# Seven block products instead of eight in two chunks of each feed-forward

## The chip, the core and the metric

One core of a Trainium2 chip runs the whole program: a launch, six transformer layers of two kinds on 256 tokens of width 1024, one output. The metric is device time in microseconds from start to end of an execution; the lower, the better. The engines of the core that matter here are TensorE (PE in the profile, with its weight loads as PEld), VectorE (DVE), ScalarE (ACT), GpSimd (POOL) and SyncE (SP), which issues nearly all loads. Each runs its own instructions in the order in which the program gives them, and waits on semaphores for the others.

## The reference, cut to what matters

The program is four layers of a first kind (mixer by short convolution, pooling or differential attention, then a feed-forward) and two of a second kind (feed-forward, mixer, feed-forward): eight feed-forwards in all. Only they change. Each is, with a root-mean-square norm ahead of it and one behind it:

```python
def _swiglu(xn, w_gate, w_up, w_down):
    return (jax.nn.silu(xn @ w_gate) * (xn @ w_up)) @ w_down
```

`xn` is 256 x 1024, `w_gate` and `w_up` are 1024 x 2816, `w_down` is 2816 x 1024, all float32.

## The kernel before, in words

A float32 product is made of three matmuls on float32r operands: every operand is split into a high part (a cast, ScalarE) and a low part (operand minus high part, VectorE), and `mm3` (line 184) adds high x high, high x low and low x high in PSUM. One matmul has a 128x128 stationary operand (tokens of one half, 128 values of k) and 128x512 moving weights; so one `mm3` is three matmuls, at lines 187 to 189.

Tokens are two halves of 128. `to_T` (line 268) transposes a half of x on TensorE, multiplies by the norm's gain (line 277) and splits it (`split`, line 193) into `xT`, a pair of large buffers; the norm's per-token factor is applied later, at the eviction of a product from PSUM.

Weights come in pieces of 128x2048 floats (1 MB; 4 blocks of k by 512 columns, or 2 by 1024 for the down product). All pieces of the program stand in one list, in the order of use (`plan_ffn`, line 321). `load_step` (line 105) issues the loads on SyncE, up to `raw_max` = 3 unsplit pieces ahead, while more than `spare` = 2 of the 19 large buffers `r8` are free. `split_step` (line 118) splits half a piece: a cast at line 134 and a subtraction at line 135. Two such steps turn a raw piece into a pair of buffers, and the raw buffer goes back.

What sets the order is `tick` (line 156): the program is written out by one thread that walks through TensorE's work, and after each `mm3` it takes one `split_step` and lets waiting tasks go on whose tick has come. A split that is not forced happens only if no `hold` is set, the piece is at most `ahead` pieces further than the one in use, fewer than `limit` pieces are split and live, and two buffers are free. `hold` is set from the end of a half's mixer or feed-forward until that half's `to_T` has been issued. `spawn(gen, n)` puts a task n ticks later, `join` forces one, `need` forces a split.

A feed-forward (`ffn`, line 337) goes through six chunks of the 2816 columns, five of 512 and one of 256. For chunk c, `gate_up(c, h)` makes gate and up of one token half in two PSUM banks (16 `mm3` each), evicts them with a Silu on ScalarE (line 368) and a product on VectorE (line 369), and spawns the task `T`, eleven ticks later, which transposes the 128x512 result on TensorE (line 375) and splits it (lines 196 and 197). `down(c, h)` multiplies it with the chunk's rows of `w_down` into two banks per half that stay open over all chunks. The loop's order is gate and up of half 0, down of the chunk before for half 1, gate and up of half 1, down of this chunk for half 0. PSUM has eight banks, and four of them are the down product's.

Behind a feed-forward or mixer, `chain` (line 296) and `post` (line 238) make the norm and the residual on ScalarE, VectorE and a power on GpSimd (line 216).

Of the kernel before, what the change touches and what calls it, by code (L numbers as in the profile page):

```python
# [27 lines left out]
ORD = "VQKvco"  # L28

# [20 lines left out]
class Core:  # L50
    def __init__(self, ctx, tc, I, out):
# [21 lines left out]
        self.raw, self.hl, self.xt = {}, {}, {}  # L73
        self.raw_max = 3
        self.spare = 2
        self.hold = 0
        self.rr = {}
# [17 lines left out]
    def add(self, *srcs):  # L95

        self.pieces.append(srcs)
        return len(self.pieces) - 1

    def view(self, t, i):  # L100
        srcs = self.pieces[i]
        kt, n = srcs[0].shape[1], sum(s.shape[2] for s in srcs)
        return t[:, 0:kt * n].rearrange("p (k n) -> p k n", k=kt)

    def load_step(self, most=10 ** 9):
        while self.n_dma < most and self.n_dma < len(self.pieces) and len(self.r8.free) > self.spare and len(self.raw) < self.raw_max:
# [8 lines left out]
            self.raw[i] = t  # L115
            self.n_dma += 1

    def split_step(self, force=False, eng=None):
        i = self.n_split
        if i >= len(self.pieces):  # L120
            return False
        if self.sub == 0:
            if not force and (self.hold or i > self.cur + self.ahead or self.live >= self.limit or len(self.r8.free) < 2):
                return False
            self.load_step()
            if i not in self.raw:
                return False
            self.hl[i] = (self.r8.get(), self.r8.get())
            self.live += 1
        hi, lo = (self.view(t, i) for t in self.hl[i])  # L130
        k = lo.shape[1]
        sl = slice(0, k // 2) if self.sub == 0 else slice(k // 2, k)
        raw = self.view(self.raw[i], i)[:, sl]
        self.nc.scalar.copy(out=hi[:, sl], in_=raw)  # L134
        (eng or self.nc.vector).tensor_tensor(out=lo[:, sl], in0=raw, in1=hi[:, sl].bitcast(F32), op=ALU.subtract)  # L135
        self.sub += 1
        if self.sub == 2:
            self.sub = 0
            self.r8.put(self.raw.pop(i))
            self.n_split += 1  # L140
            self.load_step()
        return True

    def need(self, i):
        self.cur = max(self.cur, i)
        while self.n_split <= i:
            assert self.split_step(force=True), ("no buffer for piece", i, self.n_dma, self.n_split, len(self.raw), self.raw_max, len(self.r8.free), self.sub)
        return tuple(self.view(t, i) for t in self.hl[i])
# [35 lines left out]
    def mm3(self, out, x, w, first, last, tick=True):  # L184

        mm = self.nc.tensor.matmul
        mm(out=out, lhsT=x[0], rhs=w[0], start=first, stop=False)  # L187
        mm(out=out, lhsT=x[0], rhs=w[1], start=False, stop=False)  # L188
        mm(out=out, lhsT=x[1], rhs=w[0], start=False, stop=last)  # L189
# [66 lines left out]
    def scale_of(self, h):  # L256
# [5 lines left out]
        def rest():  # L262
            r = self.sb.tile([128, 4], F32, tag=f"rr{h}", name=f"rr{h}", bufs=2)
            self.rstd(sx, 2, EPS, r)
            self.rr[h] = r[:, 1:2]
        return rest

    def to_T(self, h, gT, rest, late):
# [12 lines left out]
        for n, z in enumerate(zs):  # L281
            dst = [t[:, 0:2048].rearrange("p (k t) -> p k t", k=8)[:, 4 * n:4 * n + 4, h * 128:(h + 1) * 128] for t in self.xT]
            self.split(dst[0], dst[1], z.rearrange("p (k t) -> p k t", k=4))
            self.f2.put(z)
# [5 lines left out]
        self.spawn(last(), 3 if late else 0)  # L290
        yield
# [18 lines left out]
    def start(self, h, nxt, wait=None, late=False):  # L310
        rest = (lambda: self.scale_of(h)()) if late else self.scale_of(h)
# [4 lines left out]
        else:  # L316
            self.hold += 1
            self.xt[h] = self.spawn(self.to_T(h, self.gT, rest, late), 6 if wait is None else wait)


    def plan_ffn(self, wg, wu, wd):

        G, Dn = [], []
# [3 lines left out]
        for c in range(6):  # L327
            lo = c * 512
            if c < 5:
                G.append([self.add(w[:, 4 * q:4 * q + 4, lo:lo + 512]) for w in (gk, uk) for q in range(2)])  # L330
                Dn.append([self.add(dk[:, 4 * c + 2 * q:4 * c + 2 * q + 2, :]) for q in range(2)])
# [1111 lines left out]
```

## Time and profile before

| | |
|---|---|
| median of 3 runs | 2162.37 us (2160.11 to 2163.01) |
| the profiled execution | 2164.11 us |
| its span, first to last instruction | 2162.3 us |
| mean granted TensorE clock | 0.997 |
| busy share of TensorE, VectorE, ScalarE | 99%, 57%, 49% |
| one load of 1 MB, issue to landing | 5.1 us |

The rows further down are of this execution. In a timeline a row gives the start (us from the span's start), the time, the engine, the line, the operation, output and inputs, with a count where neighbours were merged, and in brackets how long the engine was idle before it and who released it. A matmul's row is its whole way through the array; matmuls overlap, so their cost is the distance of two starts.

### The profile page before, as it was taken

Reading aid. Unit: us, or ns where it says so; the run is one execution under the profiler, and the core shown is the slowest. Engines: PE = TensorE matmul, PEld = TensorE weight load, DVE = VectorE, ACT = ScalarE, POOL = GpSimd, SP = SyncE. Lnnn points to the kernel's source line nnn. Section 1 sums busy time; section 2 is a strip of 40 time slices with the busy share of each in tenths; the row PEclk is TensorE's granted clock in tenths of the full one; section 3 lists DMA queues with packets and bytes.
Section 4 is the critical chain, followed back from the end, with each engine's and each line's share of the span. In section 5 each row is a group of like instructions: output and inputs, shape, how many; then the busy total and the mean of one; then the engine's idle time right before and its main releaser. Section 6 shows DMA issues by size and latency. Waiting matters only on the chain.

```text
span 2162.3 us, 24820 instructions
## 1 busy us (share of the span) xinstructions
PE 2138.5 (99%) x9845; PEld 1729.2 (80%) x9845; DVE 1237.1 (57%) x1664; ACT 1066.4 (49%) x1566; POOL 82.2 (4%) x130
## 2 busy tenths in 40 slices
PE   9999999999999999999999999999999999999998
PEld 6878877887888888888888887878888888787886
DVE  6655475546665456655464554785456446477454
ACT  5554454444664435553454446764435345676342
POOL 1000010000010000000000001000000001000000
PEclk9999999999999999999999999999999999999999
DMA  8555545455454554554654554354554645345541
GB/s 295 188 201 197 190 166 179 171 196 186 137 197 163 200 189 161 210 179 156 213 189 170 193 181 142 118 193 167 196 191 150 214 171 171 128 165 175 175 176 59
DMA packets 175620, 383.73 MB, mean 177 GB/s; under 512 B 10428, under 2 KB 29116, under 8 KB 175504
## 3 DMA queue, kind: packets, MB, share of 16 engines
q1 hardware_dynamic: 172592, 372.04, 50.2%
q0 software_dynamic: 2624, 9.58, 1.2%
q8 instruction: 77, 1.26, 0.2%
q10 hardware_dynamic: 288, 0.52, 0.1%
q14 instruction: 39, 0.32, 0.0%
HBM read 380.28 MB, written 1.84 MB: 177 GB/s over the span
## 4 chain that ended last, share of the span: by engine, by line
PE 93%; DVE 3%; ACT 2%; issue 1%; POOL 1%; DMA 0%; SPq 0%; POOLq 0%; DVEq 0%; ACTq 0%
PE ps L189 29%; PE ps L188 29%; PE ps L187 29%; PE ps L206 2%; PE ps L375 2%; ACT r L134 1%; DVE r L135 1%; PE ps L1042 1%; ACT c_junk L220 1%; PE ps L687 0%; PE ps L732 0%; PE ps L783 0%; PE ps L1016 0%; ACT f L1029 0%; DMA r<-in_conv_w_in_dram 0%
## 5 line engine op out<-in xcount | busy, mean ns | idle before, releaser
L187 PE MATMUL ps<-r,r 128*128 128x512 f32 (+2 forms) x2816 | 1129.5, 401 | 2.6 <-ACT r L196 1.7
L188 PE MATMUL ps<-r,r 128*128 128x512 f32 (+2 forms) x2816 | 1108.1, 394 | 2.5 <-POOL r L135 1.4
L189 PE MATMUL ps<-r,r 128*128 128x512 f32 (+2 forms) x2816 | 1109.5, 394 | 0.1
L135 DVE TENSOR_TENSOR r<-r,r 128x1024 fp32r<-128x1024 f32 (+1 forms) x701 | 815.1, 1216 | 147.0 <-ACT r L134 140.3
L134 ACT CAST r<-r 128x1024 fp32r<-128x1024 f32 x702 | 686.0, 1041 | 194.7 <-PE ps L188 166.8
L189 PEld LDWEIGHTS ps<-r,r 128*128 128x128 f32 (+1 forms) x2816 | 528.2, 188 | 127.1 <-DVE r L197 3.8
L188 PEld LDWEIGHTS ps<-r,r 128*128 128x128 f32 (+1 forms) x2816 | 529.3, 188 | 119.3 <-DVE r L135 3.0
L187 PEld LDWEIGHTS ps<-r,r 128*128 128x128 f32 (+1 forms) x2816 | 529.3, 188 | 118.8 <-ACT r L196 2.2
L369 DVE SCALAR_TENSOR_TENSOR f<-ps,rr,f 128x512 f32<-128x512 f32 (+1 forms) x96 | 67.8, 706 | 458.6 <-PE ps L189 434.4
L196 ACT CAST r<-ps 128x512 fp32r<-128x512 f32 (+1 forms) x108 | 59.9, 555 | 456.2 <-PE ps L375 448.1
L197 DVE TENSOR_TENSOR r<-ps,r 128x512 fp32r<-128x512 f32 (+1 forms) x108 | 70.2, 651 | 189.4 <-ACT r L196 189.4
L368 ACT ACTIVATE f<-ps,rr 128x512 f32<-128x512 f32 (+1 forms) x96 | 62.6, 653 | 156.9 <-PE ps L189 156.8
L216 POOL TENSOR_TENSOR st<-st,c_mhalf 128x1 f32<-128x1 f32 x28 | 15.9, 569 | 1575.7 <-DVE st L215 1574.9
L220 ACT ACTIVATE c_junk<-x 128x512 bf16<-128x512 f32 x56 | 35.3, 631 | 51.3 <-DVE x L253 50.2
L375 PEld LDWEIGHTS ps<-c_ident,f 128*128 128x128 f32 x352 | 44.4, 140 | 13.1
L375 PE MATMUL ps<-c_ident,f 128*128 128x128 f32 x352 | 54.0, 272 | 0.0
L277 DVE TENSOR_TENSOR f<-ps,c_pre 128x512 f32<-128x512 f32 x52 | 33.8, 687 | 29.5 <-PE ps L206 29.3
L196 ACT CAST r<-f 128x512 fp32r<-128x512 f32 x52 | 31.7, 621 | 26.1 <-DVE f L277 26.0
L253 DVE SCALAR_TENSOR_TENSOR x<-f,st,x 128x512 f32<-128x512 f32 x56 | 39.6, 749 | 2.5 <-POOL st L216 0.9
L245 DVE TENSOR_TENSOR f<-ps,gn 128x512 f32<-128x512 f32 x52 | 35.5, 684 | 6.4 <-ACT c_junk L220 6.4
L220 ACT ACTIVATE c_junk<-ps 128x512 bf16<-128x512 f32 x52 | 31.0, 596 | 15.2 <-PE ps L189 14.4
L197 DVE TENSOR_TENSOR r<-f,r 128x512 fp32r<-128x512 f32 x52 | 35.6, 722 | 4.6 <-ACT r L196 2.5
(177 smaller groups left out, 749.3 us busy)
## 6 DMA issues: line engine op xcount, KB each, us to landing
r<-in_ffn_w_in_dram SPq DMA_DIRECT2D x80, 1024.0 KB, 5.2
r<-in_ffn_w_down_dram SPq DMA_DIRECT2D x44, 1024.0 KB, 5.0
r<-in_ffn_w_out_dram SPq DMA_DIRECT2D x44, 1024.0 KB, 5.1
r<-in_ffn_w_gate_dram SPq DMA_DIRECT2D x40, 1024.0 KB, 5.1
r<-in_ffn_w_up_dram SPq DMA_DIRECT2D x40, 1024.0 KB, 5.1
r<-in_mix_w_in_dram SPq DMA_DIRECT2D x28, 1024.0 KB, 5.1
r<-in_conv_w_in_dram SPq DMA_DIRECT2D x22, 1024.0 KB, 5.3
r<-in_attn_w_qkv_dram SPq DMA_DIRECT2D x12, 1024.0 KB, 5.2
```

The costliest lines, as they stand in the source:

```text
L134: self.nc.scalar.copy(out=hi[:, sl], in_=raw)
L135: (eng or self.nc.vector).tensor_tensor(out=lo[:, sl], in0=raw, in1=hi[:, sl].bitcast(F32), op=ALU.subtract)
L187: mm(out=out, lhsT=x[0], rhs=w[0], start=first, stop=False)
L188: mm(out=out, lhsT=x[0], rhs=w[1], start=False, stop=False)
L189: mm(out=out, lhsT=x[1], rhs=w[0], start=False, stop=last)
L196: self.nc.scalar.copy(out=hi, in_=src)
L197: self.nc.vector.tensor_tensor(out=lo, in0=src, in1=hi.bitcast(F32), op=ALU.subtract)
L206: self.nc.tensor.transpose(out=b[:, j * 128:(j + 1) * 128], in_=src[:, j * 128:(j + 1) * 128], identity=self.ident)
L220: self.nc.scalar.activation(out=self.junk[:, 0:src.shape[-1]], in_=src, func=ACTF.Square, scale=scale, accum_out=acc)
L368: self.nc.scalar.activation(out=s[:, 0:n], in_=gb, func=ACTF.Silu, scale=rr[h])
L369: self.nc.vector.scalar_tensor_tensor(out=s[:, 0:n], in0=ub, scalar=rr[h], in1=s[:, 0:n], op0=ALU.mult, op1=ALU.mult)
L375: self.nc.tensor.transpose(out=b[:, j * 128:(j + 1) * 128], in_=s[:, j * 128:(j + 1) * 128], identity=self.ident)
```

## The change: block products and the order of the chunks

In chunks 1 and 3 of each feed-forward gate and up are made together, as a product of two 2x2 block matrices: a11, a12, a21, a22 are the two token halves by the two halves of k, b11 and b21 the two k halves of the gate's weights, b12 and b22 of the up weights. Seven block products replace eight:

```
s1 = a21' , s2, s3, s4 : four differences of input blocks (x_sums, once per feed-forward)
t1 = b11+b12   t2 = t1+b22   t3 = b12+b22   t4 = t2+b21     (all blocks with the signs of s)
products: a11 b11, a12 b21, s1 t1, s2 t2, s4 b22, s3 t3, a22 t4, in three PSUM banks X, Z, Y
```

Each b block is loaded once and stays raw until its last use; VectorE adds blocks in place, in two halves (`pre_add`), where possible one factor ahead of the split. A list of `units` (a piece, and a piece to add to it first) takes the place of the list of pieces. The low part of a half is now issued behind the next half's cast (`lows`, `flush`). Chunk 0 keeps `gate_up`; in chunks 2 and 4 (`both`) each weight piece is used for both token halves at once, and the down product of the chunk before stands behind gate and behind up; chunk 5 is as before. `ahead` is 4 in chunk 0, then 5, then 2; `limit` is 7. The core of the diff:

```diff
+SUMS = (1, 3)
     def load_step(self, most=10 ** 9):
-        while ... len(self.r8.free) > self.spare and len(self.raw) < self.raw_max:
+        while ... len(self.r8.free) > self.spare + self.reserve and self.waiting < self.raw_max:
+    def pre_add(self, i):
+        src, first = self.units[i]
+        if first is None or i in self.summed:
+            return True
+        if src not in self.raw or first not in self.raw or any(self.units[j][0] == src for j in range(self.n_low, i)):
+            return False
...
+        for sl in (slice(0, 2), slice(2, 4)):
+            self.nc.vector.tensor_tensor(out=a[:, sl], in0=a[:, sl], in1=b[:, sl], op=ALU.add)
     def split_step(self, force=False, eng=None):
...
+            if first is not None and i not in self.summed:
+                self.flush()
+            if not force:
+                for j in range(i + 1, min(i + 2, len(self.units))):
+                    if self.units[j][1] is not None and j not in self.summed:
+                        self.pre_add(j)
+                        break
+            self.load_step()
+            if not force and (self.hold or i > self.cur + self.ahead or self.live >= self.limit or len(self.r8.free) < 2 + self.reserve):
+                self.flush()
+                self.load_step()
                 return False
...
         self.nc.scalar.copy(out=hi[:, sl], in_=raw)
-        (eng or self.nc.vector).tensor_tensor(out=lo[:, sl], in0=raw, in1=hi[:, sl].bitcast(F32), op=ALU.subtract)
+        self.lows.append((lo[:, sl], raw, hi[:, sl], eng or self.nc.vector, i, self.sub == 1))
+        self.flush(1)
+    def x_sums(self):
+        tt, stt = self.nc.vector.tensor_tensor, self.nc.vector.scalar_tensor_tensor
+        while len(self.r8.free) < 2:
+            yield 1
+        self.xs = (self.r8.get(), self.r8.get())
+        self.reserve = 0
...
+        tt(out=z[1, 1], in0=z[1, 1], in1=z[1, 0], op=ALU.subtract)
+        tt(out=z[1, 0], in0=z[0, 0], in1=z[1, 0], op=ALU.subtract)
+        put(0, z[1, 1])
+        yield 3
+        stt(out=z[0, 0], in0=z[1, 1], scalar=-1.0, in1=z[0, 0], op0=ALU.mult, op1=ALU.subtract)
+        put(3, z[1, 0])
+        yield 3
+        stt(out=z[0, 1], in0=z[0, 0], scalar=-1.0, in1=z[0, 1], op0=ALU.mult, op1=ALU.subtract)
+        put(1, z[0, 0])
+        yield 3
+        put(2, z[0, 1])
...
     def plan_ffn(self, wg, wu, wd):
+            if c in SUMS:
+                factors(c, "b11 b21 t1 t2")
+                down(c - 1, 0)
+                factors(c, "b22 t3")
+                down(c - 1, 1)
+                factors(c, "t4")
     def ffn(self, plan, half, nxt):
-        self.limit = 6
+        self.limit, self.reserve, self.ahead = 7, 2, 4
+        def both(c):
+            def half_chunk(q, use):
+                b = [self.ps.get(), self.ps.get()]
+                for i in range(2):
+                    p = G[c][2 * q + i]
+                    w = self.need(p)
+                    for h in range(2):
+                        for k in range(4):
+                            kk = 4 * i + k
+                            self.mm3(b[h], self.lhs(xT, kk, h), (w[0][:, k], w[1][:, k]), kk == 0, kk == 7)
+                        if i:
+                            self.spawn(use(h, b[h]), 1)
+                    self.done(p)
...
+            for q, use in enumerate((gate, up)):
+                half_chunk(q, use)
+                for h in range(2):
+                    down(c - 1, h, (q,))
+        def seven(c):
+            U = G[c]
+            X, Z = self.ps.get(), self.ps.get()
...
+            def product(b, n, a, first=False):
+                w = self.need(U[n])
+                for k in range(4):
+                    self.mm3(b, left[a](k), (w[0][:, k], w[1][:, k]), first and k == 0, k == 3, more=not first)
+                self.done(U[n])
...
+            product(X, "b11", "a11", True)
+            e1 = self.spawn(copy("1", X), 2)
+            product(Z, "b21", "a12", True)
+            self.join(e1)
+            e2 = self.spawn(gate0(), 2)
+            Y = self.ps.get()
+            product(Y, "t1", "s1", True)
+            e3 = self.spawn(copy("5", Y), 2)
+            product(X, "t2", "s2")
+            e4 = self.spawn(copy("2", X), 2)
+            down(c - 1, 0, (0,))
+            down(c - 1, 1, (0,))
+            self.join(e2, e3)
+            product(Y, "b22", "s4")
+            self.join(e4)
+            e5 = self.spawn(up0(), 2)
+            product(X, "t3", "s3")
+            e6 = self.spawn(up1(), 1)
+            down(c - 1, 0, (1,))
+            down(c - 1, 1, (1,))
+            self.join(e5, e6)
+            product(X, "t4", "a22")
+            if c == SUMS[-1]:
+                self.join(self.spawn(gate1()))
+            else:
+                self.spawn(gate1(), 1)
-        for c in range(5):
-            gate_up(c, 0)
-            if c:
-                down(c - 1, 1)
...
-            gate_up(c, 1)
-            down(c, 0)
+        gate_up(0, 0)
...
+        gate_up(0, 1)
+        self.join(self.st)
+        self.ahead = 5
+        for c in range(1, 5):
+            if c in SUMS:
+                seven(c)
...
+            else:
+                both(c)
...
+        self.ahead = 2
+        down(4, 0)
```

`copy` is a copy of a bank on ScalarE, `gate0` a bank add on VectorE and a Silu on ScalarE, `up0` a bank add and a product on VectorE, `up1` a bank add, `gate1` a Silu and a product; `up0` and `gate1` end with the same task `T` as before (`hidden`), twelve ticks later. `x_sums` starts two ticks after the second half's `to_T`, whose gained input blocks `z` are kept for it. In `hidden` the task also waits for a free bank and two free small buffers.

## Rows read from the trace of the kernel before

**Rows 1.** Busy time, share of the span and instructions, from the page.
```profile
PE 2138.5 (99%) x9845; PEld 1729.2 (80%) x9845; DVE 1237.1 (57%) x1664; ACT 1066.4 (49%) x1566; POOL 82.2 (4%) x130
```

**Rows 2.** Chain that ended last, share of the span by engine, from the page.
```profile
PE 93%; DVE 3%; ACT 2%; issue 1%; POOL 1%; DMA 0%; SPq 0%; POOLq 0%; DVEq 0%; ACTq 0%
```

**Rows 3.** Groups by line and form: count, busy us, mean ns, idle before and releasers.
```profile
L189 PE MATMUL ps<-r,r 128*128 128x512 f32 x2784 | 1100.0, 395 | 0.1
L135 DVE TENSOR_TENSOR r<-r,r 128x1024 fp32r<-128x1024 f32 x697 | 813.7, 1221 | 147.0 <-ACT r L134 140.3 <-PE ps L189 4.1
L134 ACT CAST r<-r 128x1024 fp32r<-128x1024 f32 x698 | 685.2, 1046 | 194.7 <-PE ps L188 166.8 <-DVE r L135 21.7 <-DMA r<-in_conv_w_in_dram 6.2
```

**Rows 4.** Timeline of PE in chunk 0, first and last of 45 matmuls.
```profile
113.69 0.39 PE L189 MATMUL ps<-r,r 128*128 128x512 f32 x1
...
123.84 0.39 PE L188 MATMUL ps<-r,r 128*128 128x512 f32 x1
```

**Rows 5.** Timeline of PE: last matmul of chunk 0; four transposes and the next matmul.
```profile
131.44 0.40 PE L189 MATMUL ps<-r,r 128*128 128x512 f32 x1
...
140.49 0.60 PE L375 MATMUL ps<-c_ident,f 128*128 128x128 f32 x4
140.85 0.48 PE L187 MATMUL ps<-r,r 128*128 128x512 f32 x1
```

**Rows 6.** Windows of chunk 0 and two later ones: stretch, length, busy by engine, clock.
```profile
108.30:130.50 22.20, 22.20 (x103) 18.04 (x102) 14.58 (x21) 12.24 (x20) 3.80 (x7) 1.00 0.59 187
...
181.40:215.70 34.30, 34.30 (x154) 27.79 (x153) 16.68 (x17) 13.99 (x16) 0.00 (x0) 1.00 0.53 184
215.70:250.10 34.40, 34.40 (x154) 27.89 (x153) 16.75 (x17) 13.99 (x16) 0.00 (x0) 1.00 0.58 200
```

**Rows 7.** Waits of VectorE: total us, times, longest.
```profile
DVE f L369 <- PE ps L189: 434.4, 71, 10.4
```

**Rows 8.** Timeline of VectorE behind the second half's input, three feed-forwards.
```profile
114.36 1.29 DVE L197 TENSOR_TENSOR r<-f,r 128x512 fp32r<-128x512 f32 x2
115.57 0.21 DVE L215 TENSOR_SCALAR rr<-st 128x1 f32<-128x1 f32 x1
115.91 6.90 DVE L135 TENSOR_TENSOR r<-r,r 128x1024 fp32r<-128x1024 f32 x6
...
635.49 6.91 DVE L135 TENSOR_TENSOR r<-r,r 128x1024 fp32r<-128x1024 f32 x6
...
1111.01 6.90 DVE L135 TENSOR_TENSOR r<-r,r 128x1024 fp32r<-128x1024 f32 x6
```

**Rows 9.** Timeline of ScalarE at the same place of the first.
```profile
114.83 5.79 ACT L134 CAST r<-r 128x1024 fp32r<-128x1024 f32 x6
```

**Rows 10.** DMA queue, from the page: packets, MB, share of 16 engines.
```profile
q1 hardware_dynamic: 172592, 372.04, 50.2%
```

**Rows 11.** Timeline of VectorE between the two halves, after the pool and both mixers.
```profile
329.27 2.36 DVE L135 TENSOR_TENSOR r<-r,r 128x1024 fp32r<-128x1024 f32 x2 [1.88 <-ACT r L134]
...
1438.36 2.36 DVE L135 TENSOR_TENSOR r<-r,r 128x1024 fp32r<-128x1024 f32 x2
...
1965.10 2.36 DVE L135 TENSOR_TENSOR r<-r,r 128x1024 fp32r<-128x1024 f32 x2
```

**Rows 12.** Windows behind a gap of PE (the clock stands after the POOL column).
```profile
316.00:318.00 2.00, 1.42 (x9) 1.21 (x9) 2.00 (x5) 1.45 (x4) 0.00 (x0) 0.75 0.00 0
318.00:320.00 2.00, 2.00 (x10) 1.83 (x9) 1.91 (x4) 1.49 (x4) 0.00 (x0) 0.50 0.00 0
320.00:322.00 2.00, 2.00 (x10) 1.62 (x9) 1.87 (x4) 2.00 (x3) 1.25 (x1) 0.90 0.66 158
```

**Rows 13.** Timeline of PE: that gap.
```profile
316.58 1.75 PE L206 MATMUL ps<-c_ident,x 128*128 128x128 f32 x8 [2.01 <-DVE x L253]
```

More of the change, by code (lines that the diff above doesn't have):

```diff
@@ L115, in load_step, with used, begin @@
             self.raw[i] = t
+            self.waiting += 1
             self.n_dma += 1
+    def used(self, i):
+        self.uses[i] -= 1
+        if not self.uses[i]:
+            self.r8.put(self.raw.pop(i))
+    def begin(self, i):
+        if i not in self.begun:
+            self.begun.add(i)
+            self.waiting -= 1
+    def pre_add(self, i):
[4 more added lines that the diff above has]
+            return False
+        self.begin(src)
+        self.begin(first)
+        a, b = (self.view(self.raw[n], src) for n in (src, first))
+        for sl in (slice(0, 2), slice(2, 4)):
+            self.nc.vector.tensor_tensor(out=a[:, sl], in0=a[:, sl], in1=b[:, sl], op=ALU.add)
+        self.used(first)
+        self.summed.add(i)
+        return True
@@ L118, in split_step, with flush @@
+    def flush(self, keep=0):
+        while len(self.lows) > keep:
+            lo, raw, hi, eng, i, last = self.lows.popleft()
+            eng.tensor_tensor(out=lo, in0=raw, in1=hi.bitcast(F32), op=ALU.subtract)
+            if last:
+                self.n_low = i + 1
+                self.used(self.units[i][0])
     def split_step(self, force=False, eng=None):
         i = self.n_split
-        if i >= len(self.pieces):
+        if i >= len(self.units):
+            self.flush()
             return False
+        src, first = self.units[i]
@@ L254, in post, with scale_of @@
         self.f2.put(*mg)
-    def scale_of(self, h):
+    def scale_of(self, h, neg=False):
         sx = self.small(4)
@@ L343, in ffn, with hidden, T @@
         hT, tt = {}, {}
+        def hidden(s, c, h, n, delay):
+            def T():
+                while not self.ps.free or len(self.r2.free) < 2:
+                    yield 1
+                b = self.ps.get()
+                for j in range(n // 128):
+                    nc.tensor.transpose(out=b[:, j * 128:(j + 1) * 128], in_=s[:, j * 128:(j + 1) * 128], identity=self.ident)
+                self.f2.put(s)
+                hT[c, h] = (self.r2.get(), self.r2.get())
+                self.split(hT[c, h][0][:, 0:n], hT[c, h][1][:, 0:n], b[:, 0:n])
+                self.ps.put(b)
+                yield
+            tt[c, h] = self.spawn(T(), delay)
         def gate_up(c, h):
@@ L651, in bias_table @@
         self.f2.put(oh)
+        while len(self.r8.free) < 2:
+            yield 1
         han = self.r8.get(F32)
```

193 lines of the change are left out of this document (142 added, 51 removed).

## The prediction

> **What bounds the kernel now.** I read the busy table first: TensorE 99%, VectorE 57%, ScalarE 49% [rows 1]. The busy time of pipelined matmuls overstates, so the chain that ended last came second: 93% of it lies on PE [rows 2]. Third, the spacing of matmuls: starts at 113.69 and 123.84 us are 44 steps apart, so one 128x512 matmul costs 10.15 / 44 = 0.231 us on the path, not the 0.395 us of its own duration [rows 3, 4]. A chunk in the middle of a feed-forward has 144 of these and eight transposes: 144 x 0.231 + 8 x 0.148 = 34.4 us (four transposes take 140.49 to 140.85 plus what the next start is late, about 0.59 us [rows 5]), which is the measured period, 34.3 and 34.4 us, with no gap [rows 6]. In the same stretches VectorE works 16.7 us and waits for the rest: its longest wait of the program is for the matmuls of the up product, 434 us [rows 6, 7]. So TensorE is the bound, and VectorE has 17 us to spare in such a chunk, but only 22.20 - 14.58 = 7.6 us in the first one, where the transposed input is also made [rows 6].
>
> **TensorE's part.** A 512-column chunk of gate and up is 2 token halves x 2 matrices x 8 k-steps x 3 = 96 matmuls. Seen as a 2x2 product (token halves x halves of k, halves of k x gate/up) it takes seven block products of 4 x 3 = 12 instead of eight: 84. Two chunks in each of eight feed-forwards: 2 x 8 x 12 = 192 matmuls fewer, 192 x 0.231 = 44.4 us off the path. Transposes, down products and the order inside the other chunks keep their count, so the turn-taking of `both` is worth nothing by itself on PE; what it does is free weight buffers earlier.
>
> The Trainium skill, TensorE: Matmul & The Clock Gate, section Back-to-back issue gap, gives N / 2.4 + 2.5 ns, 216 ns at 512 columns; the rows say 231 ns. By the page the saving would be 41.4 us; the row is of this kernel and I use it.
>
> **VectorE's part.** A half of a weight block (128x1024) is 6.90 us for six, 1.15 us each [rows 8]; an add of two blocks has the same shape and type, both operands in SBUF, so the same price. A seven-product chunk needs 14 lows instead of 8 and eight adds: 14 x 1.15 = 16.1 us more, and three bank adds at about 0.65 us (1.29 us for two of 128x512 [rows 8]), 2 us. Per feed-forward `x_sums` adds eight 128x512 operations, 5.2 us. In all 8 x (2 x 18.1 + 5.2) = 331 us on 1237: 74% of the span, on average no bound. ScalarE gets 16 x (6 casts x 0.96 us (5.79 us for six [rows 9]) + 3 copies x 0.6) + 8 x 4 x 0.62 = 141 us on 1066: not a bound either. Bytes read do not change (each block is still loaded once; the queue is at 50.2% [rows 10]).
>
> What matters is the place. In chunk 3 the preceding chunk (34 us of PE, some 17 us of VectorE) lets the factors b11, b21, t1, t2 be ready in advance, some 14 us of work; the chunk itself needs 26 halves x 1.15 + 7 small x 0.65 = 34.4 us of VectorE against 132 x 0.231 + 8 x 0.148 = 31.7 us of PE, 2.7 us more than it has, which the lead covers: nothing lost. In chunk 1 there is no such lead. I follow VectorE's program order in the first feed-forward, from the tick rules in the diff. Until both halves' inputs are transposed, splitting is held; VectorE is free at 115.8 us [rows 8]. From there to the low part of the second half's hidden block of chunk 0 (drawn eleven ticks into chunk 1; the down product that follows t2 needs it) the order has: last block of chunk 0 (2 halves), b11 (2), b21 (2), t1 (2 adds, 2 lows), t2 (4), the first down block (2), adds for t3 (2), b22 (2), t3 (2), adds for t4 (2) = 24 halves x 1.15 = 27.6 us; and 8 of `x_sums`, two up products, two hidden lows and one bank add, 13 x 0.65 = 8.4 us. In-order, it ends at 151.8 us. TensorE wants it when? Chunk 0 ends at 131.7 us [rows 5], then b11, b21, t1, t2 and the first half of the down block, 60 x 0.231 = 13.9 us, four transposes 0.6 us, two matmuls 0.5 us: 146.7 us. So TensorE is 5.1 us late there, of which about 1.3 us already falls at the last block of chunk 0, whose second low now stands behind the first three operations of `x_sums`. Behind that point VectorE has two blocks (4.6 us) to do in 16 us of PE, and it does not fall behind again.
>
> Five of the eight starts look like this one (six halves in a row right after the second input: after both convolutions, after attention, after both feed-forwards; three shown [rows 8]). After the pool and the two mixers two halves are split between the two token halves [rows 11], so 2.3 us of the queue is gone before it starts: 2.8 us late. Sum 5 x 5.1 + 3 x 2.8 = 33.9 us given back. Bounds on the lateness of one start: 0, if VectorE's order comes out so that the hidden block goes ahead of the t3, b22 and t4 work (four double halves, 9.2 us, more than the 5.1); and up to 10 us, if chunk 3 is as late as chunk 1. I take the tally itself, 4.2 us on average, as it is made of rows.
>
> ScalarE's work off the path: the low of one half is issued after the next half's cast, so the 140 us that VectorE waited for casts [rows 3] shrink; nobody was waiting for them, so zero. New waits on TensorE: X is used four times (b11, t2, t3, t4) and each reuse waits for a copy or add out of it. Between b11 and t2 lie 24 matmuls (5.5 us), between t2 and t3 36, between t3 and t4 24, against a copy of about 0.6 us: covered as long as ScalarE and VectorE are less than 5 us behind, which fails only in chunk 1, where the wait is the same lateness and is not paid twice. If that cover went in chunk 3 as well it would be the bound of 10 us above. Queued behind such a wait on PE are all matmuls; on ScalarE, behind the Silu of the first half's gate (which waits for VectorE's bank add), the hidden block's cast, counted with the tally.
>
> Sum: 2164.1 us (the profiled execution; span 2162.3 and 1.8 around it) - 44.4 + 33.9 = 2153.6; the median of the timed runs lies 1.7 us below the profiled one, so **2152 us**, 0.5% faster.
>
> **Rivals.**
> No lateness: the tally is pessimistic because the splits start earlier or the weights wait at other places. Then the whole 44.4 us come through: 2162.4 - 44.4 = 2118. For it: VectorE would be at 74% on average. Against it: chunk 0 is the one place with little room [rows 6].
> The clock falls in the wait. In this trace, behind a PE gap of 2.01 us ahead of 316.58, the granted clock read 0.75, 0.50 and 0.90 in the three windows of 2 us from 316 on [rows 12, 13], that is 1.2 GHz for a while and back to 2.4 GHz: (0.25 + 0.50 + 0.10) x 2 = 1.7 us of PE work lost. A 4 to 5 us wait in each of eight feed-forwards would add 8 x 1.7 = 13.6: 2166. Against it: while PE runs slowly VectorE catches up, and the wait may come in pieces. The Trainium skill, TensorE: Matmul & The Clock Gate, section HAM oscillation, says just this of kernels whose matmuls wait in every round: that each wait puts the array back to half rate and the price is paid each time. The rows above agree for one gap; by that rule this rival decides.
> VectorE late in both chunks (slower). Four raw blocks stay in the 19 large buffers until t3 and t4 are split, with two pairs for the input and its sums; if that stops b22 and the adds from being drawn ahead in chunk 2, chunk 3 starts without lead and is late like chunk 1. Then 2 x 33.9 = 67.8 is given back: 2162.4 - 44.4 + 67.8 = 2186. It decides as soon as the lateness per feed-forward exceeds 44.4 / 8 = 5.5 us. For it: 34.4 us of VectorE against 31.7 us of PE leaves no way to recover inside the chunk. Against it: 17 us of idle VectorE in the chunk before [rows 6].
>
> **Chances.** Forecast 0.45 (own range 2138 to 2160), no lateness 0.17, clock 0.18, late in both 0.20. Range: from near the no-lateness case to most of the late-in-both case, 2120 to 2180. What differs by less than 0.2% (4.3 us; about what a measurement of this kernel can tell from no change) is the same. Faster: all but the last hundredths of the forecast, no lateness, and a little of the clock rival: 0.62. Same: the rest of the clock rival, 0.12. Slower: late in both, and the clock rival with a larger wait: 0.26.
>
> **What would show it.** PE with 192 fewer matmuls at 0.231 us; VectorE at some 1560 us; in each feed-forward one wait of PE of some 3 to 5 us for the low of a hidden block (line of the split helper), 14 us into chunk 1, and a small one in chunk 0 for a weight's low; none in chunk 3. Chunk 1 then lasts about 35 us and chunk 3 about 31.7. The granted clock over the span stays near 0.997 in the forecast and falls by half a per cent or more in the clock rival. The forecast is wrong if chunk 1 shows no wait (then 2118), if PE waits in chunk 3 too, or if the matmul spacing itself grows with VectorE's and ScalarE's added traffic: 1% of it would cost 20 us.

## The result and the profile after

| | us | to before |
|---|---|---|
| before, median of 4 runs beside it | 2161.46 (2160.11 to 2163.01) | |
| after, median of 4 runs | 2226.23 (2219.82 to 2229.40) | 1.0296 [1.027, 1.0322] |
| mean granted clock, before and after | 0.997, 0.985 | |

The change made the kernel 3.0% slower; I had said 2152 us and a range to 2180. All times compared below are of executions in the faster of the program's two states; the profiled execution of hold_ahead3 fell in the slower one, so of that kernel only the times are used. Line numbers have moved: the three matmuls are L273 to L275, a weight's cast and low L220 and L184, a block add L176, the cast and low of a hidden block L282 and L283, bank adds L591, L597 and L605.

The busy table of the kernel after, to be read against [rows 1]: TensorE has its 192 matmuls fewer (9653 for 9845), VectorE the predicted work (1564 us), and the span is longer all the same. So the time went into waiting and, as counted below, into matmuls at a lower clock.

```profile
PE 2132.9 (96%) x9653; PEld 1704.7 (77%) x9653; DVE 1564.0 (70%) x2016; ACT 1210.6 (54%) x1742; POOL 77.8 (3%) x130
```

What TensorE waited for, after (total us, times, longest). The first row is the bank add that reads X before the last product, with t4, is added to it; the second and third are a hidden block's low and cast; the fourth is the last block of chunk 0.

```profile
PE ps L273 <- DVE f L605: 21.5, 12, 2.7
PE ps L275 <- DVE r L283: 19.9, 9, 4.7
PE ps L273 <- ACT r L282: 14.4, 16, 2.0
PE ps L274 <- DVE r L184: 13.6, 13, 1.5
```

A typical feed-forward (945.9 to 1142.8 us), all rows of PE's timeline in which it stood idle: one wait in chunk 0, three in chunk 1, one in chunk 3 (1071.00) and one towards chunk 4's end.

```profile
955.47 0.50 PE L274 MATMUL ps<-r,r 128*128 128x512 f32 x1 [1.45 <-DVE r L184]
...
984.05 0.50 PE L273 MATMUL ps<-r,r 128*128 128x512 f32 x1 [1.06 <-ACT r L282]
986.83 0.50 PE L275 MATMUL ps<-r,r 128*128 128x512 f32 x1 [2.04 <-DVE r L283]
1002.63 0.50 PE L273 MATMUL ps<-r,r 128*128 128x512 f32 x1 [2.05 <-DVE f L605]
...
1071.00 0.50 PE L273 MATMUL ps<-r,r 128*128 128x512 f32 x1 [1.95 <-DVE f L605]
...
1109.39 0.50 PE L273 MATMUL ps<-r,r 128*128 128x512 f32 x1 [0.67 <-ACT r L282]
```

I added up the distances of all matmul starts inside the eight feed-forwards. Their time went from 1524.8 to 1593.0 us, +68.2. It is made of -44.4 for the matmuls; +83.4 in gaps (distances over 0.47 us, less 0.231: 4.6 before, 88.0 after); and +28.3 in steps of 0.30 to 0.47 us, matmuls at a lower clock (10.6 and 38.9). The spacing of the rest stayed at 0.232 us. The other stages took 4 us less, which leaves the +64 of the spans.

Two more views of after say where the waits begin. ScalarE's casts and VectorE's adds wait for weights of the feed-forward to land; before, none of this was there.

```profile
ACT r L220 <- DMA r<-in_ffn_w_in_dram: 29.5, 21, 2.4
ACT r L220 <- DMA r<-in_ffn_w_down_dram: 16.8, 14, 2.3
ACT r L220 <- DMA r<-in_ffn_w_out_dram: 16.0, 13, 2.1
ACT r L220 <- DMA r<-in_ffn_w_gate_dram: 14.7, 7, 2.4
ACT r L220 <- DMA r<-in_ffn_w_up_dram: 14.2, 13, 4.6
```
```profile
DVE r L176 <- DMA r<-in_ffn_w_up_dram: 19.1, 8, 7.4
DVE r L176 <- DMA r<-in_ffn_w_in_dram: 15.1, 9, 2.1
```

And VectorE's timeline of after from the hidden block's low (L283) to the wait at 1002.63: six lows (three factors), three more behind late casts, and only then the bank adds L597 and L605. L605 ends at 1002.57; PE goes on at 1002.63.

```profile
986.09 0.68 DVE L283 TENSOR_TENSOR r<-ps,r 128x512 fp32r<-128x512 f32 x1
986.69 6.89 DVE L184 TENSOR_TENSOR r<-r,r 128x1024 fp32r<-128x1024 f32 x6
995.11 2.36 DVE L184 TENSOR_TENSOR r<-r,r 128x1024 fp32r<-128x1024 f32 x2 [1.53 <-ACT r L220]
998.22 1.22 DVE L184 TENSOR_TENSOR r<-r,r 128x1024 fp32r<-128x1024 f32 x1 [0.75 <-ACT r L220]
999.37 0.68 DVE L597 TENSOR_TENSOR f<-ps,f 128x512 f32<-128x512 f32 x1
1000.09 0.75 DVE L599 SCALAR_TENSOR_TENSOR f<-f,rr,f 128x512 f32<-128x512 f32 x1
1000.75 1.22 DVE L184 TENSOR_TENSOR r<-r,r 128x1024 fp32r<-128x1024 f32 x1
1001.89 0.68 DVE L605 TENSOR_TENSOR f<-ps,f 128x512 f32<-128x512 f32 x1
```

Two things meet in this wait. Lows stand in front of the bank adds, and VectorE stood idle for late casts, 1.53 and 0.75 us, together more than the 2.05 us that PE waited. The wait for the hidden block at 986.83 is of another kind: from 951.07 to its low at 986.09 VectorE's timeline has no gap, so no late load stands behind it.

### The profile page after: what moved, and what is told of

It is laid out like the page before. It is cut to its first block, busy times and chain, and to the rows that moved or that the text cites. A ratio compares the mean times of both kernels' runs of the same rounds, so it can differ in the third digit from the quotient of the medians.

```text
span 2226.4 us, 25069 instructions
## 1 busy us (share of the span) xinstructions
PE 2132.9 (96%) x9653; PEld 1704.7 (77%) x9653; DVE 1564.0 (70%) x2016; ACT 1210.6 (54%) x1742; POOL 77.8 (3%) x130
## 5 line engine op out<-in xcount | busy, mean ns | idle before, releaser
L273 PE MATMUL ps<-r,r 128*128 128x512 f32 (+2 forms) x2752 | 1117.5, 406 | 38.3 <-DVE f L605 21.5
L275 PE MATMUL ps<-r,r 128*128 128x512 f32 (+2 forms) x2752 | 1095.6, 398 | 20.0 <-DVE r L283 19.9
L274 PE MATMUL ps<-r,r 128*128 128x512 f32 (+2 forms) x2752 | 1091.7, 397 | 15.0 <-DVE r L184 13.6
L184 DVE TENSOR_TENSOR r<-r,r 128x1024 fp32r<-128x1024 f32 (+1 forms) x797 | 937.4, 1217 | 209.4 <-ACT r L220 198.1
L220 ACT CAST r<-r 128x1024 fp32r<-128x1024 f32 x798 | 793.6, 1042 | 360.8 <-DVE r L176 145.3
L273 PEld LDWEIGHTS ps<-r,r 128*128 128x128 f32 (+1 forms) x2752 | 523.1, 190 | 166.2 <-DVE f L605 27.0
L275 PEld LDWEIGHTS ps<-r,r 128*128 128x128 f32 (+1 forms) x2752 | 521.7, 190 | 151.9 <-DVE r L283 31.4
L274 PEld LDWEIGHTS ps<-r,r 128*128 128x128 f32 (+1 forms) x2752 | 522.9, 190 | 133.3 <-DVE r L184 21.0
L282 ACT CAST r<-ps 128x512 fp32r<-128x512 f32 (+1 forms) x108 | 59.6, 552 | 220.7 <-PE ps L498 212.4
L176 DVE TENSOR_TENSOR r<-r,r 128x1024 f32<-128x1024 f32 x128 | 150.7, 1219 | 34.2 <-DMA r<-in_ffn_w_up_dram 19.1
L283 DVE TENSOR_TENSOR r<-ps,r 128x512 fp32r<-128x512 f32 (+1 forms) x108 | 69.7, 649 | 119.9 <-ACT r L282 119.9
L558 DVE SCALAR_TENSOR_TENSOR f<-ps,rr,f 128x512 f32<-128x512 f32 x32 | 24.0, 750 | 91.0 <-PE ps L275 91.0
L282 ACT CAST r<-f 128x512 fp32r<-128x512 f32 x84 | 51.5, 621 | 48.8 <-DVE f L366 22.5
L306 ACT ACTIVATE c_junk<-x 128x512 bf16<-128x512 f32 x56 | 35.3, 631 | 54.5 <-DVE x L339 53.6
L283 DVE TENSOR_TENSOR r<-f,r 128x512 fp32r<-128x512 f32 x84 | 57.5, 709 | 4.7 <-ACT r L282 2.6
L530 DVE SCALAR_TENSOR_TENSOR f<-ps,rr,f 128x512 f32<-128x512 f32 (+1 forms) x32 | 19.7, 615 | 51.7 <-ACT f L529 51.7
L529 ACT ACTIVATE f<-ps,rr 128x512 f32<-128x512 f32 (+1 forms) x32 | 18.5, 579 | 67.9 <-PE ps L275 67.8
```

The source lines that it names most:

```text
L176: self.nc.vector.tensor_tensor(out=a[:, sl], in0=a[:, sl], in1=b[:, sl], op=ALU.add)
L184: eng.tensor_tensor(out=lo, in0=raw, in1=hi.bitcast(F32), op=ALU.subtract)
L273: mm(out=out, lhsT=x[0], rhs=w[0], start=first, stop=False, skip_group_check=more)
L274: mm(out=out, lhsT=x[0], rhs=w[1], start=False, stop=False, skip_group_check=more)
L275: mm(out=out, lhsT=x[1], rhs=w[0], start=False, stop=last, skip_group_check=more)
L282: self.nc.scalar.copy(out=hi, in_=src)
```

## The experiments

One table first; every run stood beside runs of before at 2161 to 2162 us. "Load waits" is the time in which casts and adds waited for loads of feed-forward weights (the rows as above, added up), "gaps" are PE's gaps in the feed-forwards, counted as above.

| kernel | us | ratio to before | load waits | gaps |
|---|---|---|---|---|
| before | 2161.5 | | 0 | 4.6 |
| after | 2226.2 | 1.0296 [1.027, 1.0322] | 125.4 | 88.0 |
| turns_only | 2162.7 | 1.0006 [0.9996, 1.0016] | 5.7 | 9.3 |
| third_only | 2236.3 | 1.0347 [1.0329, 1.0364] | 167.0 | 82.0 |
| add_none | 2140.6 | 0.9907 [0.9892, 0.9922] | 87.8 | 29.5 |
| add_self | 2214.8 | 1.0249 [1.0227, 1.0272] | 117.8 | 83.5 |
| turns_hold | 2184.2 | 1.0107 [1.0092, 1.0122] | 97.6 | 26.5 |
| after_limit6 | 2146.1 | 0.9929 [0.9912, 0.9945] | 0 | 30.6 |
| third_limit6 | 2163.0 | 1.0008 [0.9998, 1.0017] | 0.2 | 26.8 |
| after_settle | 2235.7 | 1.0344 [1.0328, 1.0359] | 96.2 | 97.3 |
| none_ahead3 | 2134.5 | 0.9873 [0.9859, 0.9888] | 7.1 | 22.3 |
| hold_ahead3 | 2162.5 | 1.0001 [0.9992, 1.0011] | | |
| late_sums | 2143.7 | 0.9915 [0.9899, 0.9932] | 0 | 24.7 |
| three_late | 2202.8 | 1.0189 [1.0174, 1.0205] | 0 | 84.3 |
| room3 | 2194.3 | 1.0152 [1.0137, 1.0167] | 0 | 66.5 |
| pool_ahead3 | 2251.6 | 1.0421 [1.0406, 1.0437] | 0 | 113.4 |
| two_four_late | 2125.9 | 0.9835 [0.9818, 0.9851] | 0 | 14.5 |
| two_four | 2248.0 | 1.0412 [1.0388, 1.0435] | 267.0 | 106.4 |

**First round: which part of the change.** Four kernels.

turns_only: no block products, no sums.

```diff
-SUMS = (1, 3)
+SUMS = ()
...
-        keep = nxt == "ffn"
+        keep = False
...
-        self.limit, self.reserve, self.ahead = 7, 2, 4
+        self.limit, self.reserve, self.ahead = 7, 0, 4
```

> No chunk as block products (and no sums of the input): what is left of the change is the order of the other chunks, the low part issued behind the next cast, and the new bounds for splitting. Both theories take these for free: 792 matmuls per feed-forward as before, so about 2162 us. If the turn-taking itself brings waits of TensorE (rival), it is above 2170, and the waits that cost the changed kernel 64 us are not the block products' alone.

2162.7: the turn-taking and the later lows are worth nothing, as the prediction had it.

third_only: one block product, `SUMS = (3,)`.

> Only chunk 3 as block products: 96 matmuls fewer, 22 us. Theory 1 (VectorE's time: what is late is the queue in front of the hidden block in chunk 1) expects no loss in chunk 3: 2162 - 22 + 8 x 1.5 (the low behind the input sums in chunk 0) = 2152. Theory 2 (order and buffers: VectorE's and ScalarE's work that stands in order behind blocks whose load is late, as raw blocks hold the large buffers) expects the waits of 1.2 to 2.7 us for the bank add in chunk 3 to stay, with part of the lower clock: about 2165 to 2172.

2236.3, slower than the whole change, and outside both expectations. Half of the adds gave all of the loss, and much of it lay in chunks 0 and 1, where no block was added. So the adds alone could not be the cause. What it shares with the whole change are the two large buffers of the token sums, held to the end of chunk 3.

add_none leaves the block adds out (the factors are then plain blocks); add_self adds each block to itself, so that no add waits for a second load.

```diff
-            self.nc.vector.tensor_tensor(out=a[:, sl], in0=a[:, sl], in1=b[:, sl], op=ALU.add)
```
```diff
-            self.nc.vector.tensor_tensor(out=a[:, sl], in0=a[:, sl], in1=b[:, sl], op=ALU.add)
+            self.nc.vector.tensor_tensor(out=a[:, sl], in0=a[:, sl], in1=a[:, sl], op=ALU.add)
```

> The block adds on VectorE are left out (the weight factors t1 to t4 are then plain blocks); loads, buffers, splits and matmuls stay. 128 adds, 147 us of VectorE, go. Theory 1: the waits for hidden blocks and bank adds go, the one in chunk 0 stays (8 x 1.5 us), and the lower clock goes with them: about 2135. Theory 2: only the waits for the hidden block of chunk 0 go (some 25 us and part of the clock), those for bank adds behind late loads stay: 2175 to 2195.

> Each block add takes its own block as second operand: the same instructions in the same places and the same VectorE time, but no wait for the second block's load. Theory 1: no change, 2220 to 2230. Theory 2: the 34 us that VectorE stands in adds waiting for loads go, and the waits of TensorE behind them (4.7 us in the first feed-forward, about 1 us in the others): 2205 to 2218.

2140.6 and 2214.8: of the 85.6 us that the adds cost here, 11.4 come with their second operand's load (little more than the scatter: 2211 to 2221 us against 2220 to 2229), the rest is there without it. That speaks for VectorE; third_only spoke against it. add_none still has 87.8 us of load waits on ScalarE and is faster than before all the same; what they cost it, the third round shows.

**Second round: buffers and the look-ahead.** There are 19 large buffers; the input takes two and its sums two more. With 15 left, a look-ahead of 4 to 5 factors (a pair of buffers each) leaves little for loads.

turns_hold is turns_only with two large buffers held empty, for no purpose:

```diff
+        held = (self.r8.get(), self.r8.get())
         gate_up(0, 0)
...
+            if c == 3:
+                self.r8.put(*held)
```

after_limit6 and third_limit6 shorten the look-ahead of the full change and of third_only (`limit` and `ahead` together; which of the two matters was not run):

```diff
-        self.limit, self.reserve, self.ahead = 7, 2, 4
+        self.limit, self.reserve, self.ahead = 6, 2, 3
...
-        self.ahead = 5
+        self.ahead = 3
```

after_settle holds a cast or early add back until its load is ten steps old:

```diff
+            if not force and src in self.raw and self.ticks < self.issued[src] + 10:
+                self.flush()
+                return False
```

> No block products and no adds at all: the kernel with the turn-taking alone, which ran in 2162.7, but with two of the large buffers held empty from the start of each feed-forward to the end of its chunk 3, as the token sums hold them in the full change. Theory A (with two buffers fewer the look-ahead, 7 live factors and 4 to 5 ahead, takes nearly every large buffer for hi/lo pairs, so loads are issued late and casts and lows stand in order behind loads that have not landed; the loss is one of order and buffers): 2175 to 2215. Theory B (the loss is VectorE's time for adds and sums, buffers are enough): 2162 to 2166. Rival C (buffers short only together with the four raw blocks that the adds hold): 2163 to 2172.

> The full change with a shorter look-ahead: at most 6 live factors instead of 7 and 3 ahead instead of 4 and 5, so that more large buffers are left for loads in flight; in the order in which the program hands work out, the casts then come 16 or more steps behind the issue of their load, where the full change has most of them 8 to 15 steps behind. Same arithmetic, same VectorE time. Theory A: the waits of casts and adds for loads go, and with them most of the 83 us of PE waits: 2140 to 2170. Theory B (VectorE's time): 2205 to 2230.

> The variant with one block-product chunk (chunk 3 alone, 2236.3) with the same shorter look-ahead, 6 live factors and 3 ahead. Theory A: its loss was the look-ahead, so it comes to 2150 to 2170 (the product saves 22 of 2162, the adds and sums cost 5 to 15). Theory B (VectorE's time in chunk 0 and the sums): 2215 to 2236.

> The full change with its look-ahead as it is, but a cast or an early add is not handed out before ten steps (about 7 us) have passed since its load was issued, unless the products need it at once. Buffers and arithmetic are unchanged; only casts and adds that would stand on ScalarE and VectorE waiting for a load are moved behind the other work. Theory A in its form of order (what is lost is other work queued behind casts that wait for loads): 2180 to 2205. If it is the buffers themselves (loads too late for any order): 2215 to 2230. Theory B (VectorE's time): 2220 to 2230.

Two missing buffers cost 21.5 us without a single add (turns_hold against turns_only). The shorter look-ahead takes 80.1 us off the full change and makes it faster than before, with the same arithmetic; its casts wait for no load of a feed-forward any more. third_only comes down by 73.3. SyncE's timelines show it at the same place, the fourth feed-forward: it issues its first load 18.7 us after the start in third_only (943.2 us) and 11.8 us after it in third_limit6 (912.7).

```profile
961.94 8.99 SPq L149 DMA_DIRECT2D r<-in_ffn_w_up_dram  x2
```
```profile
924.51 3.84 SPq L149 DMA_DIRECT2D r<-in_ffn_w_up_dram  x2
```

after_settle missed all of its expectations (2235.7). It took away little of what it was meant to: 96.2 of the 125.4 us of load waits are left. And the waits moved: those for chunk 0's hidden block in chunk 1 (21.6 us in after) are gone, and TensorE waits 52.9 us for the bank add alone (21.5 in after). So two readings stayed open: loads that get no buffer, or lows that stand too early in VectorE's order.

**Third round: what is left.**

```diff
-            self.st = self.spawn(self.x_sums(), 2)
+            self.st = self.spawn(self.x_sums(), 11)
```

is late_sums, on top of after_limit6; three_late is late_sums with `SUMS = (1, 2, 3)`; none_ahead3 and hold_ahead3 are add_none and turns_hold with the shorter look-ahead.

> The shorter look-ahead (6 live factors, 3 ahead, which ran in 2146.1) with the block adds left out as well; the factors are then plain blocks. With the long look-ahead the adds cost 85.6 us (2226.2 against 2140.6). Theory (the loss needs both late loads and a VectorE with no time left to catch up; with loads on time the adds fit beside the products): 2140 to 2147. Rival (VectorE's time for the adds costs something of its own in every summed chunk): 2115 to 2136.

> The turn-taking alone with two large buffers held empty, which ran in 2184.2, with the shorter look-ahead. No sums, no adds. Theory (the pairs of the look-ahead take the buffers that loads in flight need): back to 2160 to 2165. Rival (two buffers fewer cost this by themselves, whatever the look-ahead): 2178 to 2186.

> The full change with the shorter look-ahead, and the four token sums begun 11 steps after the second half's input instead of 2, so that the lows of chunk 0's last block are not queued behind them on VectorE. The wait seen there is 1.46 us in each of 8 feed-forwards. If it goes and nothing takes its place: 2133 to 2137. If VectorE is then late for the hidden block of chunk 0 or the first factor with sums: 2142 to 2155.

> late_sums with three chunks (1, 2 and 3) as block products: 96 matmuls fewer, 22 us at 0.231. VectorE was busy 28.7 and 30.6 us of the 32 in the stretches of the two summed chunks and 20.2 in the plain one between them, where it catches up. If that room is not needed: 2111 to 2118. If VectorE has no time left to catch up (my reading): 2135 to 2170, with PE waiting for VectorE in chunks 2 and 3.

hold_ahead3: 2162.5, so two missing buffers cost nothing if the look-ahead fits; with the long one they had cost 21.5 us without any add. none_ahead3: 2134.5, 6.1 us below add_none, with 7.1 us of load waits in place of 87.8; the adds cost 85.6 us with the long look-ahead and 11.6 with the short one, so most of their price was the look-ahead's, but my "nothing" was too low. late_sums gained 2.4 of the 8 x 1.46 = 11.7 us (the two intervals in the table overlap); the wait in chunk 0 went and a hidden block's cast was late in its place, 11.8 us instead of 6.9. three_late agrees with the reading that VectorE has no more time: three summed chunks in a row need it 29.5 to 30.0 us of 32, TensorE gets 28.6 to 30.6, and the kernel is 59 us slower than late_sums, more than I had expected. Three windows of three_late from the first to the last summed chunk of one feed-forward (columns as in [rows 6]):

```profile
1156.00:1188.00 32.00, 29.10 (x119) 22.64 (x118) 29.97 (x31) 18.03 (x22) 0.00 (x0) 0.95 0.56 197
1188.00:1220.00 32.00, 28.56 (x119) 22.21 (x118) 29.49 (x29) 17.81 (x21) 0.00 (x0) 0.95 0.45 164
1220.00:1252.00 32.00, 30.55 (x135) 24.22 (x134) 29.80 (x30) 21.05 (x25) 0.00 (x0) 1.00 0.54 187
```

**Fourth round: loads or order, and the place.** room3 is the full change with its long look-ahead; a cast only leaves one more buffer to the loads. pool_ahead3 is late_sums with the block adds on GpSimd, two_four_late is late_sums with `SUMS = (2, 4)`, two_four the full change with `SUMS = (2, 4)` and nothing else.

```diff
-            ... self.live >= self.limit or len(self.r8.free) < 2 + self.reserve):
+            ... self.live >= self.limit or len(self.r8.free) < 3 + self.reserve):
```

> The full change with its long look-ahead (7 live factors, 4 and 5 ahead) unchanged; only, a cast that the products don't need yet takes its pair of large buffers only if one more stays free for loads. In the order in which the work is handed out 12 casts then stand less than 12 steps behind the issue of their load, where the full change has 94. If the loss came of loads that got no buffer in time: 2142 to 2165. If it came of handing casts and lows out that many factors ahead (their place in VectorE's order): 2205 to 2230.

> late_sums (2143.7) with the block adds on GpSimd instead of VectorE; the lows stay on VectorE. If the 11.6 us that the adds cost with loads on time are VectorE's time: 2130 to 2138. If GpSimd's adds, 2.36 us a half block in the kernel before and with VectorE at less than half speed beside them, hold up the factors or VectorE: 2145 to 2200.

> late_sums with chunks 2 and 4 as block products instead of 1 and 3, so that the chunk that begins while VectorE still makes the token sums is a plain one. If the waits that are left sit where the sums meet the first block product: 2136 to 2142. If the place does not matter, or chunk 4 has too little behind it in which VectorE catches up: 2143 to 2160.

> The full change with its long look-ahead and its token sums where they were, but with chunks 2 and 4 as block products instead of 1 and 3. If the place alone makes the difference (two_four_late ran in 2125.9): 2125 to 2145. If the look-ahead costs much the same in any place (late loads, and lows queued in front of the bank evictions): 2185 to 2235.

room3 ended between its two expectations, so neither reading alone accounts for the loss. Its load waits are gone, and it is 2226.2 - 2194.3 = 31.9 us faster; the other 2194.3 - 2146.1 = 48.2 us go with the shorter look-ahead. The 31.9 us are not the loads' alone, since the spare buffer also draws fewer factors ahead: VectorE comes to the low of chunk 0's hidden block (1159.64 below) behind 18 halves of lows and adds, in after (986.09 above) behind 24, and the 21.6 us of waits for that block, where no load was late, are gone too. What is left in room3 is order. Its largest wait of PE, and VectorE's timeline ahead of one of these, both of room3:

```profile
PE ps L273 <- DVE f L605: 35.2, 16, 3.6
```
```profile
1159.64 0.68 DVE L283 TENSOR_TENSOR r<-ps,r 128x512 fp32r<-128x512 f32 x1
...
1165.92 9.52 DVE L184 TENSOR_TENSOR r<-r,r 128x1024 fp32r<-128x1024 f32 x8
1175.36 0.68 DVE L597 TENSOR_TENSOR f<-ps,f 128x512 f32<-128x512 f32 x1
1176.08 0.75 DVE L599 SCALAR_TENSOR_TENSOR f<-f,rr,f 128x512 f32<-128x512 f32 x1
1176.74 1.22 DVE L184 TENSOR_TENSOR r<-r,r 128x1024 fp32r<-128x1024 f32 x1
1177.88 0.68 DVE L605 TENSOR_TENSOR f<-ps,f 128x512 f32<-128x512 f32 x1
```

Eight lows stand in front of the bank adds, and t4's product has to wait for L605. By the list of units the last three of the eight, and the one between L599 and L605, belong to the next chunk. VectorE is busy without a break and PE waits 1.94 us. So it is at all 16 of these waits: in the 10 us up to the end of each, VectorE was busy for 9.8. The shorter look-ahead still leaves a run of six lows there, only the last of them the next chunk's, but its waits for L605 are 0.4 us at most. PE's waits in after_limit6:

```profile
PE ps L274 <- DVE r L184: 13.4, 13, 1.5
PE ps L273 <- ACT r L282: 6.9, 9, 1.5
...
PE ps L273 <- DVE f L605: 2.7, 8, 0.4
```

pool_ahead3 is the slowest of all, level with two_four within the scatter: a half block's add takes 3.14 us on GpSimd where VectorE takes 1.22, and VectorE's lows grow from 1219 to 1431 ns on average, which uses up more VectorE time (793 x 0.212 = 168 us) than the adds had taken (150.5). Groups by line of pool_ahead3, then of late_sums:

```profile
L184 DVE TENSOR_TENSOR r<-r,r 128x1024 fp32r<-128x1024 f32 x793 | 1097.2, 1431 | 160.6 <-ACT r L220 158.3
...
L176 POOL TENSOR_TENSOR r<-r,r 128x1024 f32<-128x1024 f32 x128 | 398.2, 3139 | 425.9 <-DVE r L184 425.9
```
```profile
L184 DVE TENSOR_TENSOR r<-r,r 128x1024 fp32r<-128x1024 f32 x793 | 929.8, 1219 | 136.7 <-ACT r L220 134.9
...
L176 DVE TENSOR_TENSOR r<-r,r 128x1024 f32<-128x1024 f32 x128 | 150.5, 1217 | 0.0
```

The Trainium skill, SBUF — State Buffer, section SBUF: two separate sides, says that a VectorE operation with two SBUF inputs and a GpSimd operation that reads SBUF exclude each other for the whole instruction. The trace agrees with that in its form too: 706 of the 793 lows took under 1.5 us, as all 793 do in late_sums, and 87 took over 1.8 us, 61 of them 3.2 to 3.6; the shortest adds on GpSimd took 2.3 us.

two_four_late, 2125.9, is the best version: 1.65% faster than before, 4.5% below the change as made, and 2161.2 - 2125.9 = 35.3 of the 44.4 us come through (before stood at 2161.2 beside it). In chunk 1, a plain one, VectorE now has 11 us to spare after the token sums, and each summed chunk has a plain one ahead of it. The windows of chunks 0, 1 and 2 in one feed-forward, about, of two_four_late:

```profile
1088.70:1121.00 32.30, 32.30 (x148) 25.88 (x147) 26.73 (x33) 20.21 (x28) 1.13 (x2) 1.00 0.59 212
1121.00:1153.00 32.00, 32.00 (x144) 25.94 (x143) 20.56 (x21) 14.66 (x17) 0.00 (x0) 1.00 0.39 132
1153.00:1185.00 32.00, 31.67 (x140) 25.40 (x139) 28.56 (x28) 18.75 (x22) 0.00 (x0) 1.00 0.70 254
```

two_four, the place without the look-ahead, is slower than the change (2248.0; the token sums hold their buffers until chunk 4, and load waits double to 267 us). So the place is worth something only where the buffers suffice.

## Why the prediction was wrong, step by step

- **TensorE's part, -44.4 us**: right. 192 matmuls fewer, the rest at the same spacing.
- **VectorE's sum, some 1560 us**: right (1564.0), and so was "on average no bound". (1237 + 331 is 73% of the forecast 2152 us, not 74%.)
- **The tally of VectorE's order in the first feed-forward**: right in order and time. It put the hidden block's low at 151.8 us; it ended at 151.88, and PE waited for it. I had split the lateness into 1.3 us in chunk 0 (measured 1.46) and 3.8 in chunk 1 (measured 2.04). Over all eight feed-forwards PE's waits at these two places come to 34.9 us (13.3 for L184 in chunk 0; 15.3 for L283 and 6.4 for L282 in chunk 1), where the sum had 33.9. So this term held; the loss came on top of it. PE's two rows of after, and VectorE's:

```profile
120.44 0.51 PE L274 MATMUL ps<-r,r 128*128 128x512 f32 x1 [1.46 <-DVE r L184]
...
151.94 0.65 PE L275 MATMUL ps<-r,r 128*128 128x512 f32 x1 [2.04 <-DVE r L283]
```
```profile
151.20 0.68 DVE L283 TENSOR_TENSOR r<-ps,r 128x512 fp32r<-128x512 f32 x1
```

- **"Behind that point ... it does not fall behind again", and the reuse of X "is the same lateness and is not paid twice"**: the step that failed. I counted the lows that TensorE needs next, and not those that the look-ahead draws in front of the bank adds. From the hidden block's low (986.09) to the end of L605 (1002.57) VectorE had ten halves of lows to do, 11.7 us, where I had two blocks, 4.6 us. So PE waits for L605 in 12 of the 16 summed chunks, chunk 3 too, where I had said "nothing lost": 21.5 us, the largest part of the gaps that I had put at nothing (83.4 us in all, 34.9 of them the tally's). In after, VectorE also stood idle for late casts ahead of each of the twelve, for longer than PE waited, so the two causes cannot be told apart there; room3 has the wait in all 16 with no load late, so the order is enough by itself.
- **Loads**: the working took every load as landed when its cast comes. The nearest I came was the rival of both chunks, where raw blocks in the 19 buffers stop the adds from being drawn ahead. Its place was right and its price (67.8) below the measured 83.4; its mechanism is part of what happened. In the first feed-forward an add drawn one factor ahead waits 7.44 us for its block on VectorE, with a hidden block's low queued behind it, and PE waits 4.65 us at 195.72, after:

```profile
192.70 2.36 DVE L176 TENSOR_TENSOR r<-r,r 128x1024 f32<-128x1024 f32 x2 [7.44 <-DMA r<-in_ffn_w_up_dram]
194.97 0.69 DVE L283 TENSOR_TENSOR r<-ps,r 128x512 fp32r<-128x512 f32 x1
```

- **The clock**: I put it among the rivals, at 13.6 us and as an alternative to the other mishaps. It came on top of them: 28.3 us in slow steps. Behind the gap ahead of 195.72 the granted clock read 0.50, 0.50 and 0.52 in three windows of 2 us:

```profile
194.00:196.00 2.00, 0.28 (x1) 0.29 (x2) 2.00 (x3) 0.00 (x0) 0.00 (x0) 0.50 0.00 0
196.00:198.00 2.00, 2.00 (x5) 1.53 (x5) 1.93 (x2) 0.00 (x0) 0.00 (x0) 0.50 0.00 0
198.00:200.00 2.00, 2.00 (x6) 1.60 (x5) 0.00 (x0) 0.00 (x0) 0.00 (x0) 0.52 0.00 0
```

The prediction had 1.7 us for each wait. The four rows of PE's waits above count 50 waits, but in the trace the granted clock falls to 0.50, that is 1.2 GHz, only 14 times in after, and 4 times in before; so most waits cost no clock, and 28.3 us over ten more falls are 2.8 us each, an estimate. Behind the 2.04 us ahead of 986.83 the clock stayed at 1.00. The Trainium skill, TensorE: Matmul & The Clock Gate, section HAM oscillation, has the price paid in every round of a kernel that waits for a load in each; its waits are longer than most of these, and the trace here does not show a fall at every wait.

With the terms as measured the sum closes: -44.4 + 83.4 + 28.3 - 4 for the other stages = 63 against 64 between the two spans.

What stays open: the last 9 us between two_four_late and the 2117 that the matmuls alone would give; how the loss of after divides between late loads and order; and the part of the 48 us that a better order at the long look-ahead could give back. No kernel that gives bank adds precedence over lows was run.

## What to carry over

Count what an in-order engine does between a result and the one who waits for it, look-ahead work included: work that nobody waits for yet is as good as a stall if it stands in front of a bank add that the next product waits for. When a change takes buffers, check the look-ahead's numbers against those that are left, since loads and finished operands come from one pool; and give an added load of work a place with idle time ahead of it. Several small waits are not one: each is paid, and some of them cost the clock as well.

## What the runs showed of the hardware that I had not expected

Block adds moved from VectorE to GpSimd (3.14 us against 1.22 each) made VectorE's own two-operand subtractions 17% longer on average, 1431 for 1219 ns; the rise lies in the 87 of 793 that took over 1.8 us. And the granted clock differs behind gaps of the same length: 2.04 us ahead of 151.94 was followed by windows at 0.53 and 0.61, 2.04 us ahead of 986.83 by 1.00 throughout. The runs do not say what makes the difference. Windows of after (the clock stands after the POOL column):

```profile
150.00:152.00 2.00, 0.06 (x1) 0.06 (x1) 2.00 (x4) 2.00 (x4) 0.79 (x1) 1.00 0.41 157
152.00:154.00 2.00, 2.00 (x5) 1.61 (x6) 2.00 (x2) 1.87 (x3) 0.00 (x0) 0.53 0.83 230
154.00:156.00 2.00, 2.00 (x7) 1.54 (x7) 2.00 (x3) 0.00 (x0) 0.00 (x0) 0.61 0.97 362
...
986.00:988.00 2.00, 1.17 (x5) 1.00 (x6) 2.00 (x4) 2.00 (x4) 0.00 (x0) 1.00 0.01 4
```
